# Three column blocks of the samples' token tile: high and low parts side by side as weights

## The chip, the cores and the metric

The kernel runs on one core of one Trainium2 chip. The metric is the device time of one execution in microseconds. Engines are named as in the profile: PE (TensorE, matmuls) with PEld (its weight loads), DVE (VectorE), ACT (ScalarE), POOL (GpSimd), SP (SyncE, which issues most transfers).

## The reference

One layer of a decoder trunk is applied to a prompt of 1024 positions and to a group of 8 samples with 8 positions each, with the same weights, in float32.

```python
h = rmsnorm(x, norm_mix)
q, k, v, gu, gv, ga, gb = split_in(h @ w_in)          # 1024 -> 1024|256|256|768|768|1024|1024
o = sliding-window attention of q, k, v (sinks, window 128)
vn = layernorm(gelu(gv), ln_g, ln_b)                  # an output for the samples
s = gelu(gu) * (causal 128x128 mix of vn per channel group + bias)
merged = sigmoid(ga) * (o @ w_pa) + sigmoid(gb) * (s @ w_pb)
x = x + merged @ w_out
x = x + conv_ffn(rmsnorm(x, norm_ffn))                # up 5632, causal conv 3, gelu gate, down
y = rmsnorm(x, norm_final)
```

Of the input projection, the columns v (256) and gv (768) are needed with tokens on the partitions: v for the attention's second product and for the caches, gv for the LayerNorm over its 768 channels.

## The kernel before

The 64 sample rows and 1024 prompt rows stand as columns: activations are kept transposed, with 128 channels on the partitions and tokens along the row. Every float32 operand of a large product is split into a high part, rounded to TensorE's fast float32 type, and a low part, the rest (`split`, `scale_split`: a cast on ACT, a subtraction on DVE). A product then takes three passes: high by high, high by low, low by high; low by low is left out.

The tokens form two groups. Group 0 has the 64 samples and prompt rows 0 to 511 (576 columns), group 1 the other 512 prompt rows. `hs[k]` holds group 0's normalised input without the row factor (high and low part, 576 columns) for each of the eight 128-channel chunks k. Eight such pairs lie in the first three of four tile pairs `txa[0][kk]`; the fourth pair is written only after group 0's blocks, by `split0(3)`.

The blocks v and gv (as gv0, gv1, gv2, of 256 columns each) are computed with tokens as TensorE's weights and the split weight columns (`wide[key]`, tiles `w2h`, `w2l`, two slots) as the moving operand, so that a result tile has 128 tokens on the partitions and 256 columns. Group 0 has five token tiles, the first named "s" at column 0: it takes 128 columns, of which the first 64 are the samples and the rest prompt rows 0 to 63, which the next tile computes as well. The kernel uses the first 64 rows of it alone. Group 1 has four.

The order at the start is: gv0 of group 0, chunk by chunk as input and weights arrive (`mm_tok` for all five tiles of a chunk, L612); then `tokens(0, "gv1")`, `tokens(0, "v")`, `tokens(0, "gv2")`, and for group 1 v, gv2, gv0, gv1. After the first tile of gv1, `stats_first` computes the row factors `rstg[0]` (a matmul of summed squares with ones at L475, DVE at L257, POOL's power at L258, and diagonals on DVE at L484), and applies Gelu to gv0's five banks. After every token tile one of a list of jobs runs on ACT and DVE: squares, group 1's normalised rows (`norm1`), sums and splits for the later products. A tile's bank (`bank()`, seven of them in turn) is read by ACT in `v_out` or `gv_out`, with the row factor as scale, and stored to DRAM (`gvd`, `vsd`).

Later, while the rest of the input projection runs (seven products in place of eight of 2x2 blocks, `Chain.product`, L300), `ln_load`, `ln_stats` and `ln_out` take the gv rows back from DRAM, one token tile after another, normalise them and store them by channel group (`vnd`) for the mix; the samples' 64 rows also go to the output `gvs`.

Each engine works through its own instructions in order. The instruction order of an engine is set when the program is built, from the order of the code and a planner's idea of when operands are ready; it is not strictly that of the code. Transfers are issued by SP and ACT.

Of the kernel before, what the change touches and what calls it, by code (L numbers as in the profile page):

```python
# [6 lines left out]
F32 = mybir.dt.float32  # L7
F32R = mybir.dt.float32r
I32 = mybir.dt.int32
AF = mybir.ActivationFunctionType  # L10
ALU = mybir.AluOpType
# [4 lines left out]
P = 128  # L16
D = 1024
KD = 8
NS = 64
# [6 lines left out]
GW = 768  # L26
# [8 lines left out]
def layer(tc, a):  # L35
    nc = tc.nc
    V, S, G, PE = nc.vector, nc.scalar, nc.gpsimd, nc.tensor

    def split(hi, lo, src):
        S.copy(hi, src)  # L40
        V.tensor_sub(lo, src, hi.bitcast(F32))  # L41
# [5 lines left out]
    with ExitStack() as top:  # L47
# [19 lines left out]
        eps, warm, mhalf, sign = two[:, 0:1], two[:, 1:2], two[:, 2:7], two[:, 7:8]  # L67
# [252 lines left out]
        def pick(x, place, lo, hi):  # L320
# [3 lines left out]
        groups = [dict(g=0, n=576, off=0, soff=NS, base=192, mbase=448, blk0=0,  # L324
                       chunks=[(192, 0, 320), (512, 320, 576)],
                       toks=[("s", 0), *((i, NS + P * i) for i in range(4))]),
                  dict(g=1, n=512, off=576, soff=0, base=0, mbase=0, blk0=4,
                       chunks=[(0, 0, 256), (256, 256, 512)], toks=[(4 + i, P * i) for i in range(4)])]
# [15 lines left out]
        gvd = {name: dr(f"gvd{name}", [P, GW]) for gr in groups for name, _ in gr["toks"]}  # L344
        vnd = [dr(f"vnd{gr['g']}", [P, NG, len(gr["toks"]), P]) for gr in groups]
# [12 lines left out]
        with ExitStack() as ph1:  # L358
            c1 = ph1.enter_context(tc.tile_pool(name="c1", bufs=1))

            def const1(name, shape, dt=F32):
                t = c1.tile(shape, dt, name="c_" + name)
                nc.sync.dma_start(t, a[name])
                return t
# [6 lines left out]
            late = {}  # L371

            def load_late():
                nc.sync.dma_start(ident, a["ident"])
                late["mprev"] = const1("mprev", [P, 1, P], I32)
                late["sinkb"] = const1("sinkb", [P, NH])
                late["sinks"] = const1("sinks", [P, NKV])
                neg = c1.tile([P, 1], F32, name="c_neg")
                V.memset(neg, NEG)
                late["neg"] = neg  # L380
                w2 = c1.tile([NS, NG, NS], F32, name="c_wss")
                w2r = stg.tile([P, 576], F32, name="stg")[:NS, :NG * NS]
                nc.sync.dma_start(w2r, a["wss"])
                m2 = stg.tile([P, 576], F32, name="stg")[:NS, :NG * NS].bitcast(I32)
                nc.sync.dma_start(m2, a["mss"])
                w2f = w2.rearrange("p a b -> p (a b)")
                V.memset(w2f, 0.0)
                V.copy_predicated(w2f, m2, w2r)
                late["wss"] = w2

            wide = {}
# [71 lines left out]
            rstg = [c1.tile([P, len(gr["toks"])], F32, name=f"rst{gr['g']}") for gr in groups]  # L463
# [40 lines left out]
            gvp = pa0.enter_context(tc.tile_pool(name="gvp", bufs=3))  # L504
            wide["pool"] = pa0.enter_context(tc.tile_pool(name="wide", bufs=2))
            gap(wide["pool"], 192)
            hs, txa = [], [{}, {}]
# [15 lines left out]
            def part1(t, k, lo):  # L523

                return t[:, 5 + lo // 256 if k > 3 else 4 * (lo // 256), lo % 256:lo % 256 + P]

            def mm_tok(ps, g, lo, w, k):
                wh, wl = w
                ah, al = ((part1(t, k, lo) for t in txa[1][k % 4]) if g else (t[:, lo:lo + P] for t in hs[k]))
                for i, (u, v) in enumerate(((ah, wh), (ah, wl), (al, wh))):  # L530
                    PE.matmul(ps, u, v[:, k, :], start=k + i == 0,  # L531
                              stop=k == KD - 1 and i == 2)

            def v_out(g, i, ps):
                name = groups[g]["toks"][i][0]
                v = gvp.tile([P, 256], F32, name="gv")
                S.activation(v, ps, AF.Copy, scale=1.0 if g else rstg[g][:, i:i + 1])
                if name == "s":
                    nc.sync.dma_start(vsd, v[0:NS])
                    for b in range(8):  # L540
                        nc.sync.dma_start(a["vsn"][b], v[8 * b:8 * b + 8])
                else:
                    if name == 4:
                        late["v"] = gvp.tile([P, 256], F32, name="gv")
                        nc.sync.dma_start(late["v"], v3d)
                    for to, x in ((vd, v), (dvd, None)):
                        if x is None and name == 0:
                            continue
                        t = W.sm.tile([P, 4, P], F32, name="ws", bufs=2)
                        tr, four = t.bitcast(F32R), lambda y: y.rearrange("p (h d) -> p h d", d=64)  # L550
                        if x is None:
                            x = t[:, :, 64:128]
                            V.tensor_sub(x, four(v), four(late["v"]))
                            scale_split(tr[:, :, 0:64], tr[:, :, 64:128], x, sign)
                        else:
                            split(tr[:, :, 0:64], tr[:, :, 64:128], four(x))
                        nc.sync.dma_start(to[name], t)
                    late["v"] = v
                    if name == 3:
                        nc.sync.dma_start(v3d, v)  # L560
                if name == 7:
                    nc.sync.dma_start(a["vp"], v)

            def gv_out(g, i, p3, ps, v=None):
                if v is None:
                    v = gvp.tile([P, 256], F32, name="gv")
                S.activation(v, ps, AF.Gelu_apprx_tanh, scale=1.0 if g else rstg[g][:, i:i + 1])
                nc.scalar.dma_start(gvd[groups[g]["toks"][i][0]][:, 256 * p3:256 * p3 + 256], v)

            def tokens(g, key, out, jobs, new=True, after=None):  # L570
                if new:
                    W.get()
                    W.get()
                for i, (_, lo) in enumerate(groups[g]["toks"]):
                    ps = bank()[:, :256]
                    for k in range(KD):
                        mm_tok(ps, g, lo, wide[key], k)
                    if after and i == 0:
                        after()
                    out(i, ps)  # L580
                    if jobs:
                        jobs.pop(0)()
# [16 lines left out]
            ps = bank()  # L599
# [18 lines left out]
                    V.tensor_add(rsg[0], xk[0] if k == 1 else rsg[0], x)  # L618
            with tc.issue_after(dma.ins):
                load_late()  # L620
            rows, first_gv = {}, []

            def stats_first():
# [117 lines left out]
            lnv, lnm = {}, {}  # L741

            def ln_load(n):
                if n < len(lnn):
                    if "lnp" not in late:
                        lnp = late["lnp"] = poola("ln", 1, lno)
                        for x in ("lng", "lnb"):
                            late[x] = lnp.tile([P, GW], F32, name=x)
                            nc.sync.dma_start(late[x], a[x])
                    g, i = lnn[n]  # L750
                    lnv[n] = late["lnp"].tile([P, GW], F32, name="v", bufs=4)
                    nc.sync.dma_start(lnv[n], gvd[groups[g]["toks"][i][0]])

            def ln_stats(n):
                lnp, v = late["lnp"], lnv[n]
                bs_ = lnp.tile([P, 2, 6], F32, name="bst", bufs=2)
                for e in range(2):
                    V.bn_stats(bs_[:, e], v[:, e * 384:e * 384 + 384])
                mv = lnm[n] = lnp.tile([P, 3], F32, name="mv", bufs=3)
                V.bn_aggr(mv[:, 0:2], bs_)  # L760
                V.tensor_scalar(mv[:, 2:3], mv[:, 1:2], EPS, None, ALU.add)
                G.tensor_tensor(mv[:, 2:3], mv[:, 2:3], mhalf[:, 0:1], ALU.pow)

            def ln_out(n):
                (g, i), v, mv = lnn[n], lnv.pop(n), lnm.pop(n)
                V.scalar_tensor_tensor(v, v, mv[:, 0:1], late["lng"], ALU.subtract, ALU.mult)
                V.scalar_tensor_tensor(v, v, mv[:, 2:3], late["lnb"], ALU.mult, ALU.add)
                nc.sync.dma_start(vnd[g][:, :, i], v.rearrange("p (g c) -> p g c", c=P))
                if groups[g]["toks"][i][0] == "s":
                    nc.sync.dma_start(a["gvs"], v[0:NS])  # L770

            def ln_half(n, e):
                def go():
# [625 lines left out]
            for c in range(KD):  # L1399
                for at, go in enumerate(merge(1, c, operand(1)) if c > 1 else [none, none, *first[c][2:]]):  # L1400
                    if at == 1:
                        t, u = held.pop(c)
# [36 lines left out]
            for c in range(KD):  # L1439
                xt = x_next(0, c)  # L1440
                w, ps = W.get(), acc2()
# [66 lines left out]
            for c in range(KD):  # L1508
                xt = x_next(1, c)
                w, ps = W.get(1 if c < 7 else 4), acc2()  # L1510
# [490 lines left out]
```

## Time and profile before

| | |
|---|---|
| median of 3 runs | 1510.91 us (1510.36 to 1510.93) |
| profiled execution | 1509.93 us, of which span 1508.2 us |
| PE busy | 1493.7 us, 99% of the span, 12190 matmuls |
| DVE busy | 1158.7 us, 77% |
| ACT busy | 825.9 us, 55% |
| POOL busy | 265.8 us, 18% |
| mean transfer rate | 190 GB/s |
| mean granted clock of TensorE | 0.998 |

A row of the order of time has the start in us from the span's beginning, the duration, the engine, the line of the kernel, the operation, output tile and input tiles, shapes and a count (rows of like instructions in sequence are merged); in brackets stands how long the engine sat idle before it and what ended that. Rows of waits have the waiting engine, tile and line, the one it waited for, total us, times, and the longest. Rows of windows have the stretch, its length, the busy time and count of instructions running in it, the granted clock, the share of the transfer engines and GB/s. Rows of groups have a count, the busy time with the mean in ns of one, and the idle time before them. A row of one line's instructions gives the shortest, median and longest duration in ns. A matmul's duration is its latency: matmuls overlap, and the distance of their starts is what counts.

### The profile page before, as it was taken

To read this page: it belongs to the slowest core of one execution; us is meant where nothing else is said; L and a number is where in the kernel's file an instruction comes from. 1 tells how busy PE (TensorE), PEld (TensorE's weight loads), DVE (VectorE), ACT (ScalarE), POOL (GpSimd) and SP (SyncE) were. 2 spreads that over 40 slices of the span, in tenths; PEclk is the share of its full clock that TensorE was granted. 3 is DMA by queue.
4 is the path that set the end of the run, shared out by engine and by line. 5 is a ranking of instruction groups with operands and counts; after the bars stand their busy time and mean duration, and the time that the engine had idled before them with its cause. 6 is when DMAs were issued, how large, how long until landed. Compare 5 with 4: busy or idle time off the path is not lost.

```text
span 1508.2 us, 31375 instructions
## 1 busy us (share of the span) xinstructions
PE 1493.7 (99%) x12190; PEld 1481.7 (98%) x12190; DVE 1158.7 (77%) x1909; ACT 825.9 (55%) x1755; POOL 265.8 (18%) x422
## 2 busy tenths in 40 slices
PE   9999999999999999999999999999999999999997
PEld 9999999999999999999999999999999999999997
DVE  6896778756645995989668888898899888785685
ACT  6665764544543774874434555555555556453463
POOL 0000012200120331530222322322132122000002
PEclk9999999999999999999999999999999999999999
DMA  8452457637749757849978333332233226973453
GB/s 289 157 188 112 179 177 265 228 126 271 243 167 333 249 181 224 254 160 322 342 257 282 129 115 122 117 117 107 98 136 109 91 74 219 367 259 97 123 183 133
DMA packets 137508, 286.70 MB, mean 190 GB/s; under 512 B 15248, under 2 KB 44368, under 8 KB 137360
## 3 DMA queue, kind: packets, MB, share of 16 engines
q1 hardware_dynamic: 132352, 279.97, 55.2%
q10 hardware_dynamic: 5008, 4.73, 0.9%
q8 instruction: 96, 1.57, 0.4%
q14 instruction: 52, 0.43, 0.1%
HBM read 195.76 MB, written 90.85 MB: 190 GB/s over the span
## 4 chain that ended last, share of the span: by engine, by line
PE 76%; DVE 5%; ACT 2%; issue 1%; DMA 1%; POOL 0%; DVEq 0%; ACTq 0%; POOLq 0%
PE st L300 41%; PE dn L1740 15%; PE mm L240 14%; PE sc L1233 1%; PE mx L841 1%; PE po L1294 1%; ACT s L1256 1%; DVE s L1259 1%; DVE s L1243 1%; DVE nm L1249 1%; PE pt L1266 1%; DVE of L1305 0%; DVE wl L41 0%; DVE pl L41 0%; DMA v<-gvd 0%
## 5 line engine op out<-in xcount | busy, mean ns | idle before, releaser
L300 PE MATMUL st<-th,wh 128*128 128x256 f32 (+1 forms) x2128 | 610.6, 287 | 1.2 <-ACT ku L283 0.8
L300 PE MATMUL st<-tl,wh 128*128 128x256 f32 (+1 forms) x2128 | 608.7, 286 | 0.0
L300 PE MATMUL st<-th,wl 128*128 128x256 f32 (+1 forms) x2128 | 608.2, 286 | 0.0
L300 PEld LDWEIGHTS st<-th,wh 128*128 128x128 f32 x2128 | 399.9, 188 | 2.6 <-ACT k L281 1.2
L300 PEld LDWEIGHTS st<-th,wl 128*128 128x128 f32 x2128 | 400.3, 188 | 0.0
L300 PEld LDWEIGHTS st<-tl,wh 128*128 128x128 f32 x2128 | 399.7, 188 | 0.0
L40 ACT CAST wh<-wraw 128x512 fp32r<-128x512 f32 (+2 forms) x204 | 139.4, 694 | 99.7 <-PE st L300 35.3
L41 DVE TENSOR_TENSOR wl<-wraw,wh 128x512 fp32r<-128x512 f32 (+2 forms) x204 | 158.5, 790 | 40.2 <-ACT wh L40 38.3
L1740 PE MATMUL dn<-th,wh 128*128 128x288 f32 (+1 forms) x616 | 176.7, 287 | 0.0
L1740 PE MATMUL dn<-tl,wh 128*128 128x288 f32 (+1 forms) x616 | 176.2, 286 | 0.0
L1740 PE MATMUL dn<-th,wl 128*128 128x288 f32 (+1 forms) x616 | 175.1, 284 | 0.0
L40 ACT CAST wh<-ws 128x512 fp32r<-128x512 f32 x160 | 98.1, 622 | 99.8 <-PE st L300 65.5
L41 DVE TENSOR_TENSOR wl<-ws,wh 128x512 fp32r<-128x512 f32 x160 | 111.1, 707 | 44.1 <-ACT wh L40 42.1
L1740 PEld LDWEIGHTS dn<-th,wl 128*128 128x128 f32 x616 | 115.8, 188 | 0.0
L1740 PEld LDWEIGHTS dn<-tl,wh 128*128 128x128 f32 x616 | 115.7, 188 | 0.0
L1740 PEld LDWEIGHTS dn<-th,wh 128*128 128x128 f32 x616 | 115.6, 188 | 0.0
L288 POOL TENSOR_TENSOR z<-ku,k 128x256 f32<-128x256 f32 (+1 forms) x32 | 29.5, 926 | 316.7 <-ACT ku L283 315.4
L41 DVE TENSOR_TENSOR tl<-traw,th 128x544 fp32r<-128x544 f32 (+1 forms) x85 | 61.4, 730 | 22.9 <-ACT th L40 22.8
L40 ACT CAST th<-traw 128x544 fp32r<-128x544 f32 (+1 forms) x85 | 53.8, 642 | 43.9 <-PE dn L1740 28.6
L240 PE MATMUL mm<-s,wh 128*128 128x256 f32 (+1 forms) x384 | 76.7, 294 | 0.0
L531 PE MATMUL st<-w2h,th 128*128 128x256 f32 x308 | 74.5, 283 | 0.2 <-DVE w2l L165 0.2
L240 PE MATMUL mm<-oh,wh 128*128 128x256 f32 (+1 forms) x256 | 73.5, 288 | 0.2
(300 smaller groups left out, 3157.9 us busy)
## 6 DMA issues: line engine op xcount, KB each, us to landing
wraw<-wt SPq DMA_DIRECT2D x133, 512.0 KB
traw<-td SPq DMA_DIRECT2D x77, 272.0 KB
td<-za SPq DMA_DIRECT2D x22, 544.0 KB
wraw<-wt SPq DMA_DIRECT2D x35, 256.0 KB
upd<-hl SPq DMA_DIRECT2D x14, 512.0 KB
td<-t SPq DMA_DIRECT2D x11, 544.0 KB
qd<-q SPq DMA_DIRECT2D x8, 576.0 KB
q<-qd SPq DMA_DIRECT2D x8, 576.0 KB
```

The source lines that it names most:

```text
L40: S.copy(hi, src)
L41: V.tensor_sub(lo, src, hi.bitcast(F32))
L240: PE.matmul(ps[:, lo:lo + c1 - c0], u[:, k, :], v[:, c0:c1], start=(clear and k == 0 and i == 0), stop=(k == nk - 1 and i == 2), skip_grou ...
L288: op(to, pick(x, to, lo, hi), pick(y, to, lo, hi))
L300: PE.matmul(ps, u[:, kk, :], v, start=first and kk + i == 0, stop=kk == 3 and i == 2, skip_group_check=True)
L531: PE.matmul(ps, u, v[:, k, :], start=k + i == 0, stop=k == KD - 1 and i == 2)
L841: PE.matmul(ps[:, P * i:P * i + P], vn[:, i], late["wst"][:, c, :], start=True, stop=True)
L1233: PE.matmul(ps[:, h, o0:256], q, kst[kv][:, e, k0:cur + P], start=e == 0, stop=e == 1)
L1243: V.copy_predicated(s[:, :, 0:P], late["mprev"].to_broadcast([P, 4, P]), ps[:, :, 0:P])
L1249: V.tensor_reduce(nm, s, AX.X, ALU.max, negate=True)
L1256: S.activation(s[:, h], s[:, h], AF.Exp, bias=nm[:, h:h + 1], accum_out=dn[:, h:h + 1])
L1740: PE.matmul(place(m, e), u[:, m, :], v[:, lo:hi], start=new and i + k == 0 and (e == 0 or m % 2 == 0), stop=i == NU - 1 and k == 2, skip_g ...
```

## The change

The samples' tile of three column blocks (gv1, v and gv2 of group 0; gv0 stays) takes other weights: a tile `pair_s` of 8 chunks x 128 columns, in which columns 0 to 63 are the high parts of the 64 samples and columns 64 to 127 the low parts. POOL fills it with sixteen copies of 128x64 from `hs`; it lies in the high tile of the pair `txa[0][3]`. The tile is computed in two passes (by the weights' high part and by their low part) in place of three. Its result has the samples' high-part rows on partitions 0 to 63 and their low-part rows on 64 to 127: `joined` copies the upper rows from PSUM to partitions 0 to 63 on ACT and adds the lower ones on DVE. ACT's activation then reads the sum, on 64 partitions. The sample tile's transfers to and from DRAM and its LayerNorm instructions are cut to 64 rows. The low-by-low product is now part of these three blocks for the samples.

```diff
+            def joined(ps):
+
+                t = gvp.tile([P, 256], F32, name="gv")[0:NS]
+                S.copy(t, ps[NS:P])
+                V.tensor_add(t, t, ps[0:NS])
+                return t
+
             def v_out(g, i, ps):
                 name = groups[g]["toks"][i][0]
-                v = gvp.tile([P, 256], F32, name="gv")
-                S.activation(v, ps, AF.Copy, scale=1.0 if g else rstg[g][:, i:i + 1])
+                if name == "s":
+                    v = joined(ps)
+                    S.activation(v, v, AF.Copy, scale=rstg[g][0:NS, i:i + 1])
+                else:
+                    v = gvp.tile([P, 256], F32, name="gv")
+                    S.activation(v, ps, AF.Copy, scale=1.0 if g else rstg[g][:, i:i + 1])
...
             def gv_out(g, i, p3, ps, v=None):
-                if v is None:
+                name = groups[g]["toks"][i][0]
+                m = NS if name == "s" else P
+                if name == "s" and p3:
+                    v = ps = joined(ps)
+                elif v is None:
                     v = gvp.tile([P, 256], F32, name="gv")
-                S.activation(v, ps, AF.Gelu_apprx_tanh, scale=1.0 if g else rstg[g][:, i:i + 1])
-                nc.scalar.dma_start(gvd[groups[g]["toks"][i][0]][:, 256 * p3:256 * p3 + 256], v)
+                S.activation(v[0:m], ps[0:m], AF.Gelu_apprx_tanh, scale=1.0 if g else rstg[g][0:m, i:i + 1])
+                nc.scalar.dma_start(gvd[name][0:m, 256 * p3:256 * p3 + 256], v[0:m])
...
-                for i, (_, lo) in enumerate(groups[g]["toks"]):
+                for i, (name, lo) in enumerate(groups[g]["toks"]):
                     ps = bank()[:, :256]
                     for k in range(KD):
-                        mm_tok(ps, g, lo, wide[key], k)
+                        if name != "s":
+                            mm_tok(ps, g, lo, wide[key], k)
+                            continue
+                        for e in range(2):
+                            PE.matmul(ps, pair_s[:, k], wide[key][e][:, k, :], start=k + e == 0,
+                                      stop=k == KD - 1 and e == 1)
...
             with tc.issue_after(dma.ins):
                 load_late()
+            pair_s = txa[0][3][0].rearrange("p j c -> p (j c)")[:, 0:KD * P].rearrange("p (k c) -> p k c", c=P)
+            for k, x in enumerate(hs):
+                for e in range(2):
+                    G.tensor_copy(pair_s[:, k, 64 * e:64 * e + 64], x[e][:, 0:NS])
...
-                    lnv[n] = late["lnp"].tile([P, GW], F32, name="v", bufs=4)
-                    nc.sync.dma_start(lnv[n], gvd[groups[g]["toks"][i][0]])
+                    m = NS if groups[g]["toks"][i][0] == "s" else P
+                    lnv[n] = late["lnp"].tile([P, GW], F32, name="v", bufs=4)[0:m]
+                    nc.sync.dma_start(lnv[n], gvd[groups[g]["toks"][i][0]][0:m])
...
```

`ln_stats` and `ln_out` are cut to the same `m` partitions in each of their instructions, and `ln_out` stores 64 rows of `vnd` for the samples' tile.

More of the change, by code (lines that the diff above doesn't have):

```diff
@@ L750, in ln_load @@
                     g, i = lnn[n]
-                    lnv[n] = late["lnp"].tile([P, GW], F32, name="v", bufs=4)
-                    nc.sync.dma_start(lnv[n], gvd[groups[g]["toks"][i][0]])
+                    m = NS if groups[g]["toks"][i][0] == "s" else P
+                    lnv[n] = late["lnp"].tile([P, GW], F32, name="v", bufs=4)[0:m]
+                    nc.sync.dma_start(lnv[n], gvd[groups[g]["toks"][i][0]][0:m])
             def ln_stats(n):
                 lnp, v = late["lnp"], lnv[n]
-                bs_ = lnp.tile([P, 2, 6], F32, name="bst", bufs=2)
+                m = v.shape[0]
+                bs_ = lnp.tile([P, 2, 6], F32, name="bst", bufs=2)[0:m]
                 for e in range(2):
                     V.bn_stats(bs_[:, e], v[:, e * 384:e * 384 + 384])
-                mv = lnm[n] = lnp.tile([P, 3], F32, name="mv", bufs=3)
+                mv = lnm[n] = lnp.tile([P, 3], F32, name="mv", bufs=3)[0:m]
                 V.bn_aggr(mv[:, 0:2], bs_)
                 V.tensor_scalar(mv[:, 2:3], mv[:, 1:2], EPS, None, ALU.add)
-                G.tensor_tensor(mv[:, 2:3], mv[:, 2:3], mhalf[:, 0:1], ALU.pow)
+                G.tensor_tensor(mv[:, 2:3], mv[:, 2:3], mhalf[0:m, 0:1], ALU.pow)
             def ln_out(n):
                 (g, i), v, mv = lnn[n], lnv.pop(n), lnm.pop(n)
[L766 to L770, printed above, removed]
+                m = v.shape[0]
+                V.scalar_tensor_tensor(v, v, mv[:, 0:1], late["lng"][0:m], ALU.subtract, ALU.mult)
+                V.scalar_tensor_tensor(v, v, mv[:, 2:3], late["lnb"][0:m], ALU.mult, ALU.add)
+                nc.sync.dma_start(vnd[g][0:m, :, i], v.rearrange("p (g c) -> p g c", c=P))
+                if m == NS:
+                    nc.sync.dma_start(a["gvs"], v)
             def ln_half(n, e):
```

## The prediction

> **What bounds the kernel now.** I read the page's busy table and slices first, then TensorE's waits, then windows and the order of time in the stage that the edit touches.
>
> ```profile
> span 1508.2 us, 31375 instructions
> PE 1493.7 (99%) x12190; PEld 1481.7 (98%) x12190; DVE 1158.7 (77%) x1909; ACT 825.9 (55%) x1755; POOL 265.8 (18%) x422
> PE   9999999999999999999999999999999999999997
> PEclk9999999999999999999999999999999999999999
> ```
> ```profile
> PE st L601 <- DVE c_ones L75: 1.2, 1, 1.2
> PE po L1294 <- ACT s L1241: 1.1, 1, 1.1
> ...
> PE st L300 <- ACT ku L283: 0.8, 1, 0.8
> PE fs L1775 <- ACT sq L1759: 0.6, 1, 0.6
> PE st L531 <- ACT tl L44: 0.6, 1, 0.6
> ...
> PE st L531 <- DVE w2l L165: 0.2, 1, 0.2
> ```
>
> TensorE is the bound in every slice, and its longest wait anywhere is 1.2 us. So a matmul that goes is worth its spacing in the stream, wherever it stands, and time saved early is kept: no later stage has a large wait that would soak it up. By the same rows a delay of TensorE's start is paid in full.
>
> The page's 276 to 287 ns of one matmul are latency; the spacing comes from windows.
>
> ```profile
> 14.59:21.17 6.58, 6.58 (x59) 1.00 0.98 295
> ...
> 46.80:115.10 68.30, 68.30 (x583) 1.00 0.56 181
> ```
>
> The first window has 58 starts beside one matmul already running: 6.58 / 58 = 0.113 us. The second, the same kind of matmul for most of it, gives 68.30 / 581 = 0.118 us at the same granted clock of 1.00.
>
> **The terms that leave.** The samples' tile has 8 chunks in three passes, 24 matmuls; now 16. Three column blocks (gv1, v, gv2 of group 0) lose 8 each; gv0 keeps its three passes. The tiles of gv1 and v stand where the spacing is 0.113: 8 x 0.113 = 0.91 us each. That of gv2 starts near 53 us, where it is 0.118: 0.94 us. Sum 2.76 us, or 0.18%. The number of columns loaded as weights stays 128, so the weight loads go with their matmuls and cost nothing apart.
>
> **What comes in at the start: sixteen copies on POOL.** The side-by-side tile is filled from the split rows of chunk k, two copies of 128x64 each. POOL itself has the room:
>
> ```profile
> 25.52 1.17 POOL L258 TENSOR_TENSOR rst<-rst,c_eps 128x5 f32<-128x5 f32 x1 [24.49 <-DVE rst L257]
> ```
>
> It sits idle for 24.49 us before its first real instruction. The nearest copies of that length are at L913 (64 elements in a row), some with VectorE idle, some with it busy:
>
> ```profile
> L913 POOL COPY qs<-stg x16: 229/234/742, 439.2 to 445.1; 64x64 f32<-64x64 f32 x16
> ...
> 439.25 2.15 POOL L913 COPY qs<-stg 64x64 f32<-64x64 f32 x8 [1.48 <-PE st L300]
> 441.44 4.33 POOL L913 COPY qs<-stg 64x64 f32<-64x64 f32 x8
> 441.54 0.69 DVE L41 TENSOR_TENSOR wl<-wraw,wh 128x512 fp32r<-128x512 f32 x1 [3.06 <-ACT wh L40]
> 442.32 0.69 DVE L41 TENSOR_TENSOR wl<-ws,wh 128x512 fp32r<-128x512 f32 x1
> 443.05 0.69 DVE L179 TENSOR_TENSOR ws<-ws,wraw 128x512 f32<-128x512 f32 x1
> ...
> 63.41 0.68 DVE L41 TENSOR_TENSOR tl<-wh,th 128x512 fp32r<-128x512 f32 x1
> 64.01 0.42 DVE L669 SCALAR_TENSOR_TENSOR wl<-stg,wh 128x256 f32<-128x256 f32 x1
> ```
>
> Alone, eight copies take 2.15 us, 0.27 each. Beside VectorE subtractions of two SBUF operands the next eight take 4.33 us. The subtractions pay too: their starts are 441.54, 442.32, 443.05, so 0.78 and 0.73 us apart, where 63.41 to 64.01 shows 0.60 with POOL idle. A copy that slips in between two such instructions costs VectorE 0.13 to 0.18 us.
>
> That matters because VectorE, not TensorE, gates the first tile of gv1:
>
> ```profile
> 10.40 0.81 DVE L45 SCALAR_TENSOR_TENSOR tl<-wh,c_gains,tl 128x576 fp32r<-128x576 f32 x1
> ...
> 13.73 0.81 DVE L45 SCALAR_TENSOR_TENSOR tl<-wh,c_gains,th 128x576 fp32r<-128x576 f32 x1
> ...
> 16.59 0.81 DVE L45 SCALAR_TENSOR_TENSOR tl<-wl,c_gains,th 128x576 fp32r<-128x576 f32 x1
> 17.32 0.75 DVE L618 TENSOR_TENSOR rs<-rs,wh 128x576 f32<-128x576 f32 x1
> 18.17 0.76 DVE L618 TENSOR_TENSOR rs<-rs,wl 128x576 f32<-128x576 f32 x1
> 18.85 2.35 DVE L41 TENSOR_TENSOR w2l<-wraw,w2h 128x1024 fp32r<-128x1024 f32 x2
> 21.12 0.75 DVE L618 TENSOR_TENSOR rs<-rs,wh 128x576 f32<-128x576 f32 x1
> ```
> ```profile
> 14.60 0.39 PE L531 MATMUL st<-w2h,tl 128*128 128x256 f32 x1
> ...
> 21.18 0.28 PE L531 MATMUL st<-w2h,th 128*128 128x256 f32 x1
> 21.29 0.35 PE L531 MATMUL st<-w2l,th 128*128 128x256 f32 x1
> ```
>
> From 10.4 us VectorE runs without a gap: low parts of h for chunks 2 to 7 (10.40 is chunk 2, 13.73 chunk 4, 16.59 chunk 7), sums of squares, and at 18.85 the two halves of gv1's low weights, done at 21.20. TensorE reads them with the tile's second matmul, at 21.29: no slack. The new tile has the same order (high weights first, low second) and waits for the same instruction.
>
> All of these subtractions have two SBUF operands. Copies of chunks 0 and 1 fall before 10 us, where VectorE waits for others. Those of chunks 2 to 7, twelve, become ready between about 10.4 and 19 us, one or two per chunk, and go in one per gap between VectorE's instructions; from 10.40 to the second half at 18.85 there are fourteen such gaps, so I let all twelve in. The cost is 12 x 0.13 = 1.6 to 12 x 0.18 = 2.2 us; I take 12 x 0.15 = 1.8. Ends of the unknown: nothing, if the copies find gaps; 12 x 0.23 = 2.8, if VectorE loses each copy's whole duration (0.23 is the L913 copies' median). Part of it shows at 14.60 already, where TensorE follows chunk 4's low part by 0.06 us: five copies earlier, 0.75 us. That delay lies inside the 1.8, since the weights come later still.
>
> [...]
>
> **What else comes in.** The tile's result is joined: ACT copies rows 64 to 127 of PSUM, VectorE adds rows 0 to 63, then ACT's activation on 64 rows as before. So ACT waits for VectorE once per block, with its next Gelu or cast behind it, and VectorE waits for ACT, with its next split behind it.
>
> ```profile
> L281 ACT COPY k<-st 128x256 f32<-128x256 f32 x76 | 27.5, 366 | 9.1 <-PE st L300 8.6 <-ACT gv L567 0.4
> ...
> 445.59 0.41 DVE L288 TENSOR_TENSOR z<-ku,st 128x256 f32<-128x256 f32 x1
> ...
> 26.72 0.84 ACT L567 ACTIVATE wl<-st,rst 128x256 f32<-128x256 f32 x2 [3.77 <-POOL rst L258]
> ...
> 33.09 1.23 DVE L41 TENSOR_TENSOR w2l<-wraw,w2h 128x1024 fp32r<-128x1024 f32 x1 [5.34 <-ACT w2h L40]
> ...
> 67.22 0.28 PE L531 MATMUL st<-w2h,th 128*128 128x256 f32 x1
> ```
>
> That is 0.37 and 0.41 us per block. In gv1 it lies in ACT's 3.77 us of idleness before 26.72 and VectorE's 5.34 before 33.09: nothing. In v and gv2 it lies beside TensorE's stream. The next thing that TensorE needs is group 1's operands: the last splits of its normalised rows are at 63.41 (done 64.09), used from 67.22, a cover of 3.1 us; three added blocks of 0.8 us at most, in an engine pair that recovers between them, and TensorE arriving 1 us earlier, leave it covered. If that cover were gone, the excess would be paid one to one. The bank of the tile is asked for again seven tiles later: nothing.
>
> The scratch tile for the pair is the fourth high tile of group 0, whose own contents are written after group 0's blocks; nothing waits. The sample tile's rows written to and read from DRAM halve (ACT's and SP's queues carry as many transfers, smaller), and the LayerNorm instructions run on 64 partitions with the same elements per partition: nothing.
>
> **Sum.** +1.8 - 0.91 - 0.91 - 0.94 = -0.96 us. The profiled execution took 1509.93 us (span 1508.2 and 1.7 around it) and would take about 1509.0; the median of the runs shown, 1510.91, is 0.98 above it, and moves to 1509.95.
>
> **Rivals.**
> - *The copies cost VectorE nothing on the path* (they find gaps, or VectorE yields nothing). For it: half the copies at L913 ran at 0.27. Against: the 0.73 and 0.78. Then -2.76: 1508.15. Chance 0.20.
> - *VectorE loses each copy in full*: 2.8 - 2.76, no change, 1510.95. For it: the eight copies' doubling; against: the spacing. Chance 0.18.
> - *TensorE's spacing between 46 and 115 us changes.* The 0.118 sets in with no wait and no clock change behind it, so a shifted start may fall on 0.113: 581 x (0.1176 - 0.1134) = 2.4 us more gained, 1507.5. Against: nothing in the order of matmuls there changes. Chance 0.10.
> - *POOL starves, and the new tile waits for its copies: slower.* If VectorE's unbroken run kept POOL out, the twelve copies would start in its first gap, near 24.4 us, and be done 12 x 0.27 = 3.3 us later; the tile would end near 27.9 instead of 23.99, +3.9, then -0.91 - 0.94: +2.05, 1512.95. It decides for slower once gv1's tile starts over 2.76 us late. Against: at 441.44 to 443.05 one copy got in per subtraction. Chance 0.07.
> - Forecast 0.42; another order of the work on ACT and VectorE, either way, 0.03.
>
> **How the numbers follow.** 0.2% is 3.02 us, about what a measurement of this kernel can tell from no change; the whole gain of the matmuls is below it. Faster by more: the spacing's rival, and the first rival with a little besides, 0.10 + 0.04. Slower by more: starvation worse than worked out, and the unnamed, 0.04 + 0.03. The rest, 0.79, is within. The range runs from the first rival to somewhat above the second, 1508.0 to 1511.6: with the forecast these hold 0.80.
>
> **What the profile would show.** Right: gv1's first sample matmul near 22 us and its second near 23.1, with a wait of TensorE for w2l at L41 of about 1 us; VectorE's 128x576 instructions 0.85 to 0.9 us apart between 10 and 20 us, instead of 0.73; POOL copies of 0.6 to 0.8 us there; 16 matmuls in each of three sample tiles; group 1's first matmul near 66.2. Wrong: gv1's sample tile starting by 21.4 (first rival), a wait of TensorE for a POOL copy (starvation), or another spacing after 46 us. A new wait of TensorE in v or gv2 for a bank or for group 1's operands would mean that joining the rows was not covered.

## The result: 2.6 us slower, and the profile after

The changed kernel took 1513.99 us (median of 13 executions, 1511.05 to 1515.74), the kernel before beside it 1510.66 us (13, 1509.05 to 1512.43). The ratio is 1.0017, 95% interval [1.0010, 1.0024]: by the ratio 2.6 us slower (the medians lie 3.3 us apart), where 0.96 us faster was forecast. Two later comparisons of the same two kernels gave 1.0014 [1.0004, 1.0023] and 1.0016 [1.0006, 1.0025].

The profiled execution of after took 1515.74 us, the upper end of its range, while that of before, 1509.93, stood 0.7 below its median; so the two traces lie 5.8 us apart, more than the medians. First the page's busy table:

```profile
span 1514.0 us, 31353 instructions
PE 1495.1 (99%) x12166; PEld 1481.9 (98%) x12166; DVE 1159.4 (77%) x1912; ACT 829.7 (55%) x1758; POOL 277.3 (18%) x438
```

Then the longest of TensorE's waits in the same execution (waiting engine, tile and line, releaser: total us, times, longest):

```profile
PE st L531 <- DVE w2l L41: 2.6, 1, 2.6
...
PE sc L1168 <- issue: 0.7, 1, 0.7
```

The 24 matmuls are gone (12166 against 12190), POOL has its 16 copies more (438 against 422), ACT and DVE 3 more each. New is a wait of TensorE of 2.6 us for the low weights `w2l` at L41. Before, no wait for them at that line is listed; the 0.2 us for `w2l` in the list of before is of L165, at the kernel's start. TensorE in the order of time around it (start, duration, engine, line, tiles; in brackets the idle time before and its releaser):

```profile
98.17 0.28 PE L531 MATMUL st<-w2h,tl 128*128 128x256 f32 x1
98.70 0.38 PE L531 MATMUL st<-w2h,th 128*128 128x256 f32 x1 [0.25 <-ACT w2h L40]
101.69 0.38 PE L531 MATMUL st<-w2l,th 128*128 128x256 f32 x1 [2.61 <-DVE w2l L41]
...
102.41 0.42 PE L531 MATMUL st<-w2h,tl 128*128 128x256 f32 x1
102.62 0.41 PE L531 MATMUL st<-w2h,th 128*128 128x256 f32 x1
...
105.18 0.41 PE L531 MATMUL st<-w2h,th 128*128 128x256 f32 x1
105.40 0.32 PE L531 MATMUL st<-w2l,th 128*128 128x256 f32 x1
105.56 0.28 PE L531 MATMUL st<-w2h,tl 128*128 128x256 f32 x1
105.68 0.28 PE L531 MATMUL st<-w2h,th 128*128 128x256 f32 x1
```

This is group 1's last column block, gv1, with its weights split anew. TensorE waits there for the second half of `w2l`, and then its matmuls stand 0.21 us apart until 105.4 us, instead of 0.12. The windows show the granted clock (length; busy us and count of PE, PEld, DVE, ACT, POOL; granted clock, transfer share, GB/s):

```profile
101.00:104.00 3.00, 2.31 (x12) 2.31 (x13) 3.00 (x5) 0.99 (x3) 0.00 (x0) 0.68 0.67 202
104.00:107.00 3.00, 3.00 (x22) 3.00 (x22) 3.00 (x8) 2.45 (x5) 0.00 (x0) 0.76 0.30 115
```

So in this execution the stage costs twice: the wait itself, and then some 16 spacings of 0.211 instead of 0.118, another 1.5 us.

Where does the time go? I set the start of each TensorE matmul against the start of the same matmul in the trace before (negative: earlier). All kernels of this study, each explained further down, stand in one table, the columns being times of the trace before (101.2 is the last matmul ahead of the first that needs the second half of `w2l`). The last two columns are of that block and the start of the next stage alone:

| kernel | 56 us | 101.2 | 122 | 300 | 480 | end | wait for `w2l` | half clock behind a wait near 100 to 116 us |
|---|---|---|---|---|---|---|---|---|
| after | -2.85 | -2.44 | +1.67 | +2.99 | +4.01 | +5.3 | 2.6 | 3.4 us |
| again | -3.07 | -2.94 | +1.17 | +1.95 | +2.72 | +2.8 | 2.6 | none |
| again2 | -3.24 | -3.24 | +0.11 | +0.76 | +1.56 | +3.3 | 2.0 | none |
| swap | -2.69 | -2.69 | +3.85 | +3.48 | +4.59 | +4.8 | 0.3 | 6.8 us |
| third | -0.43 | -0.43 | +0.35 | +0.21 | +1.53 | +1.3 | under 0.2 | none |
| twice | +2.61 | +2.61 | +7.03 | +7.41 | +8.51 | +11.2 | 2.5 | 3.4 us |
| drop | -3.53 | -3.53 | -0.13 | -0.06 | +0.03 | +0.3 | 1.8 | 3.4 us |
| buf4 | -2.93 | -2.93 | -3.17 | -3.80 | -2.95 | -1.8 | under 0.2 | none |
| buf4_2 | -1.82 | -1.81 | -0.79 | +0.72 | +1.53 | +2.4 | under 0.2 | none |
| dropb | -2.09 | -2.09 | -2.32 | -3.71 | -3.70 | -2.6 | under 0.2 | none |
| buf4b | -0.32 | -0.32 | -0.26 | -1.34 | -1.24 | +1.0 | under 0.2 | none |
| rows64 | +0.05 | +0.05 | +0.03 | -1.07 | -1.07 | 0.0 | under 0.2 | none |

By 56 us the change has given what its matmuls are worth, 2.85 us (2.76 was worked out). It keeps that until 98 us, and by 104 us stands 2.1 us behind. One traced execution differs from the next: rows64, which hardly changes anything, shifts by 1.1 us and back, and after, again and again2, one and the same kernel, end up to 2.5 us apart. So single entries beyond 122 us say less than the step between 101.2 and 122.

### The profile page after: what moved, and what is told of

Same layout as the page of the kernel before. It is cut to its first block, busy times and chain, and to the rows that moved or that the text cites. A ratio compares the mean times of both kernels' runs of the same rounds, so it can differ in the third digit from the quotient of the medians.

```text
span 1514.0 us, 31353 instructions
## 1 busy us (share of the span) xinstructions
PE 1495.1 (99%) x12166; PEld 1481.9 (98%) x12166; DVE 1159.4 (77%) x1912; ACT 829.7 (55%) x1758; POOL 277.3 (18%) x438
## 3 DMA queue, kind: packets, MB, share of 16 engines
q8 instruction: 95, 1.56, 0.4%
## 4 chain that ended last, share of the span: by engine, by line
PE 87%; DVE 8%; ACT 2%; DMA 2%; issue 1%; SPq 0%; DVEq 0%; ACTq 0%
PE st L300 50%; PE dn L1767 15%; PE mm L240 14%; PE st L531 3%; PE sc L1260 1%; ACT s L1283 1%; PE mx L868 1%; DVE s L1286 1%; DMA gvd<-gv 1%; PE po L1321 1%; DVE wl L41 1%; DVE tl L41 1%; DVE s L1270 1%; DVE nm L1276 1%; DVE of L1332 0%
## 5 line engine op out<-in xcount | busy, mean ns | idle before, releaser
L41 DVE TENSOR_TENSOR wl<-wraw,wh 128x512 fp32r<-128x512 f32 (+2 forms) x204 | 160.2, 798 | 36.0 <-ACT wh L40 34.1
L41 DVE TENSOR_TENSOR wl<-ws,wh 128x512 fp32r<-128x512 f32 x160 | 109.2, 695 | 50.8 <-ACT wh L40 49.2
L41 DVE TENSOR_TENSOR tl<-traw,th 128x544 fp32r<-128x544 f32 (+1 forms) x85 | 61.3, 730 | 22.4 <-ACT th L40 22.3
L240 PE MATMUL mm<-ol,wh 128*128 128x256 f32 (+1 forms) x256 | 74.1, 290 | 0.0
```

The source lines that it names most:

```text
L240: PE.matmul(ps[:, lo:lo + c1 - c0], u[:, k, :], v[:, c0:c1], start=(clear and k == 0 and i == 0), stop=(k == nk - 1 and i == 2), skip_grou ...
```

## Who makes the weights late

The weights `w2l` are a VectorE subtraction behind a cast on ACT. First the trace before, then the trace after, ACT and DVE between 82 and 102 us:

```profile
90.63 0.38 ACT L567 ACTIVATE gv<-st 128x256 f32<-128x256 f32 x1 [2.81 <-DMA gvd<-gv]
...
94.91 2.00 ACT L40 CAST w2h<-wraw 128x1024 fp32r<-128x1024 f32 x2
96.74 2.35 DVE L41 TENSOR_TENSOR w2l<-wraw,w2h 128x1024 fp32r<-128x1024 f32 x2
101.25 0.28 PE L531 MATMUL st<-w2l,th 128*128 128x256 f32 x1
```
```profile
83.10 0.34 ACTq L583 DMA_DIRECT2D gvd<-gv  x1
84.53 0.68 ACT L40 CAST th<-wh 128x576 fp32r<-128x576 f32 x1 [1.46 <-DVE wh L720]
89.43 0.39 ACT L582 ACTIVATE gv<-st 128x256 f32<-128x256 f32 x1 [4.23 <-DMA gvd<-gv]
...
93.48 0.39 ACT L582 ACTIVATE gv<-st 128x256 f32<-128x256 f32 x1 [2.02 <-DMA gvd<-gv]
...
94.88 1.04 ACT L40 CAST w2h<-wraw 128x1024 fp32r<-128x1024 f32 x1
95.81 0.67 ACT L40 CAST th<-wh 128x576 fp32r<-128x576 f32 x1
97.02 0.68 ACT L40 CAST th<-wl 128x576 fp32r<-128x576 f32 x1 [0.53 <-DVE wl L693]
97.60 1.04 ACT L40 CAST w2h<-wraw 128x1024 fp32r<-128x1024 f32 x1
...
96.90 1.22 DVE L41 TENSOR_TENSOR w2l<-wraw,w2h 128x1024 fp32r<-128x1024 f32 x1
...
100.41 1.22 DVE L41 TENSOR_TENSOR w2l<-wraw,w2h 128x1024 fp32r<-128x1024 f32 x1
```

Before, both halves were done at 96.74 + 2.35 = 99.09 and needed at 101.25: 2.2 us to spare, less than the 2.85 us by which TensorE now comes earlier. But the weights came later as well, at 100.41 + 1.22 = 101.63. Two things on ACT stand ahead of this; the runs below show which of them counts. Gelu writes gv rows into a ring of three buffers (`gvp`), and ACT writes a buffer again only when its store to DRAM has landed: the Gelus at 89.43 and 93.48 us each start 0.08 us behind a landing (89.35, 93.40). Two of the three still hold v rows here, whose difference DVE takes at 91.59 (L564), so Gelu has one in effect. TensorE delivers earlier, and the store goes out 1.9 us earlier (83.10; before at 85.04), but by the semaphores of its sixteen transfer engines it lands at 89.35, only 1.2 us before the 90.55 of the trace before; the next one, issued at 89.84, lands at 93.40. ACT stands still for 4.2 + 2.0 us instead of 2.8, with every cast queued behind. And the two halves of the weights, next to each other before, now have split0(2)'s casts between them (on DVE 98.41 to 100.41). The instruction orders are fixed when the program is built, and the order after differs from that before.

## The experiments

**rows64.** The kernel before with the LayerNorm's cut alone.

```diff
-                S.activation(v, ps, AF.Gelu_apprx_tanh, scale=...)
-                nc.scalar.dma_start(gvd[name][:, 256 * p3:...], v)
+                S.activation(v[0:m], ps[0:m], AF.Gelu_apprx_tanh, scale=...)
+                nc.scalar.dma_start(gvd[name][0:m, 256 * p3:...], v[0:m])
```

> The kernel before with the cut to 64 rows alone (the samples' Gelu, transfers and LayerNorm instructions of gv; three passes as before). Every theory: no new wait of TensorE and a time within 1 us of before.

Measured in one profiled execution: 1509.94 us, end shift 0.0, no new wait. The trace shows neither a cost nor a gain of the cut, as the prediction had it; one execution can't tell a microsecond.

**twice.** The changed kernel with POOL's copies done twice over.

```diff
-                for e in range(2):
+                for e in (0, 1, 0, 1):
                     G.tensor_copy(pair_s[:, k, 64 * e:64 * e + 64], x[e][:, 0:NS])
```

> Each of the sixteen copies is made twice. By the prediction's price (0.13 to 0.18 us of VectorE per copy between two subtractions) the low weights of group 0's gv1 would be done about 2 us later than in the changed kernel, near 23.1 us, and gv1's second matmul would wait that long. By the changed kernel's trace (about 0.02 us per copy) they are done within 0.5 us of 21.1, unless POOL itself finishes its copies after TensorE asks for them.

One profiled execution took 1521.08 us. POOL's copies in the order of time:

```profile
18.38 2.40 POOL L644 CAST th<-th 128x64 fp32r<-128x64 f32 x2
...
22.33 2.03 POOL L644 CAST th<-th 128x64 fp32r<-128x64 f32 x3
24.30 0.54 POOL L644 CAST th<-tl 128x64 fp32r<-128x64 f32 x2
```

And one of TensorE's waits:

```profile
PE st L596 <- POOL th L644: 1.9, 2, 1.5
```

VectorE was not late: gv1's tile reached its low weights at 20.74 us, 0.5 us earlier than in the trace before. The cost showed at POOL itself, whose last copies ended near 24.8 us and for which TensorE then waited 1.9 us; 6.8 us at half the granted clock followed, from 25.6 us on. The copies' price for VectorE, the disputed term, is thereby nearly nothing, and the prediction's fourth rival (the tile waits for POOL) is real once the copies are doubled. In the kernel as changed they were done at 18.9 us, before TensorE's 20.98.

**swap.** In the list of jobs after each token tile, split0(2) and the empty job behind it change places, so that the casts for gv1's second half are queued ahead.

```diff
-                    ..., split0(1), both(x_in(3), sums0(2)), split0(2),
-                    none, both(ahead(1), sums0(3)), ...
+                    ..., split0(1), both(x_in(3), sums0(2)), none,
+                    split0(2), both(ahead(1), sums0(3)), ...
```

> One entry of the list of jobs moves: split0(2) and the empty job behind it change places, so that both halves of gv1's weights for group 1 stand ahead of that split in the code. Theory (the order that the planner made of ACT's and VectorE's work puts the second half behind other splits): the wait of 2.6 us falls under 0.7 us, no half clock follows, and the time is 3 to 4.5 us under the changed kernel's, 1508 to 1510. Rival (TensorE arrives 2.85 us early at a stage that transfers and ACT's waits hold to its own time, whatever the order): the wait stays above 2 us and the time at 1512 to 1515.

Measured: 1515.07 us, above the 1508 to 1510 expected, ratio to before 1.0019 [1.0009, 1.0029]. TensorE's waits in its profile:

```profile
PE st L300 <- ACT k L281: 3.6, 2, 3.4
...
PE st L531 <- DVE w2l L41: 0.3, 1, 0.3
```

Its windows behind that wait:

```profile
112.00:116.00 4.00, 0.96 (x9) 0.75 (x7) 3.97 (x8) 3.60 (x10) 0.00 (x0) 0.94 0.66 182
116.00:119.00 3.00, 2.65 (x12) 2.65 (x13) 1.60 (x3) 0.57 (x2) 0.00 (x0) 0.50 0.61 238
119.00:122.50 3.50, 3.50 (x19) 3.50 (x18) 0.42 (x1) 0.37 (x1) 0.00 (x0) 0.52 0.00 0
```

The wait for `w2l` is down to 0.3 us as meant, and the lead is lost some 14 us later, in a wait of 3.4 us for ACT's first copy of the next stage, with 6.8 us of half clock around and behind it. ACT is no later there than in the changed kernel, whose first copy of that stage came at 116.54, 116.03 and 114.98 us in three executions (after, again, again2). The rows of swap, then of again:

```profile
115.92 0.65 ACT L281 COPY k<-st 128x256 f32<-128x256 f32 x2 [0.40 <-ACT gv L582]
...
116.03 0.65 ACT L281 COPY k<-st 128x256 f32<-128x256 f32 x2 [0.40 <-ACT gv L582]
```

So ACT comes there about as late in both, and TensorE, where it has not lost its lead to the weights, loses it to the copy. The order of the two halves decides where the lead is lost, not whether. My theory that the order was the cause fell here.

**third.** The changed kernel with a third matmul per chunk, so that TensorE has no lead.

```diff
-                        for e in range(2):
-                            PE.matmul(ps, pair_s[:, k], wide[key][e][:, k, :], start=k + e == 0,
-                                      stop=k == KD - 1 and e == 1)
+                        for e in range(3):
+                            PE.matmul(ps, pair_s[:, k], wide[key][e % 2][:, k, :], start=k + e == 0,
+                                      stop=k == KD - 1 and e == 2)
```

> The samples' tile gets a third matmul per chunk again (the high weights a second time, so that this product is counted twice): TensorE has as many matmuls as before, all else is the changed kernel's. If TensorE's lead is what uncovers the weights, the wait at group 1's gv1 falls to 0 to 0.5 us, without half clock, and the time is 1510.5 to 1511.5. If the weights come late by the order alone, moving with TensorE, the wait stays at 2 us or more and the time is 1514 to 1518.

In the profile TensorE does not wait for these weights at all without the lead, and ACT's store wait is back to one, of 3.0 us; so far the first of the two expectations holds. Its time does not: 1514.97 us, from 1511.6 to 1520.6, ratio 1.0025 [1.0012, 1.0039]. With as many matmuls as before and no lead to lose, the changed kernel is still slower than before. The profiled execution, 1511.73, was near the low end, so what the others lost is not seen.

**drop.** The other way round: the kernel before with the lead and nothing added.

```diff
-                        mm_tok(ps, g, lo, wide[key], k)
+                        mm_tok(ps, g, lo, wide[key], k, 2 if g + i == 0 else 3)
```

> The kernel before, in which the samples' tile of gv1, v and gv2 leaves out its third pass (the samples' low parts by the high weights): 24 matmuls fewer, and nothing added: no copies on POOL, no joining, no 64-row tiles. Theory (the lead itself is lost at the stage's end): TensorE is 2.7 us ahead near 56 us and loses 2 us or more of it by 116 us in waits for gv1's low weights or for the first product's bank; 1510 to 1514. Rival (the added instructions of the change are what delays ACT and VectorE): no wait, and 1508 to 1509, 2.7 us under before.

Measured: 1512.64 us, ratio 1.0004 [0.9992, 1.0015]. Twenty-four matmuls less, and no gain that the interval shows. From its profile, TensorE's longest wait and ACT's:

```profile
PE st L531 <- DVE w2l L41: 1.8, 1, 1.8
...
ACT gv L567 <- DMA gvd<-gv: 5.4, 2, 3.4
```

And the windows there:

```profile
98.00:101.00 3.00, 1.32 (x9) 1.33 (x10) 3.00 (x5) 0.36 (x3) 0.00 (x0) 0.93 0.70 190
101.00:104.00 3.00, 3.00 (x16) 3.00 (x15) 3.00 (x8) 2.46 (x5) 0.00 (x0) 0.50 0.73 288
```

A lead of 3.5 us at 101.2 is 0.1 at 122. This is the cleanest run of the study: no copies on POOL, no joined rows, and the lead is lost at the same place. With three buffers for gv rows, the lead itself can't pass this stage.

**buf4 and buf4b.** A fourth buffer for gv rows, so that ACT need not wait for the stores, in the changed kernel (buf4) and in the kernel before (buf4b). The room for it comes from loading the mask `c_wss` in `mix_first` instead of at the start.

```diff
-            gvp = pa0.enter_context(tc.tile_pool(name="gvp", bufs=3))
+            gvp = pa0.enter_context(tc.tile_pool(name="gvp", bufs=4))
...
-                w2 = c1.tile([NS, NG, NS], F32, name="c_wss")     # at the start
+                w2 = mp.tile([NS, NG, NS], F32, name="c_wss")     # in mix_first
```

> The changed kernel with four gv buffers in place of three (the mask tile c_wss, which stood in that room, is loaded later). In the changed kernel ACT stood still 4.2 and 2.0 us near 89 and 93 us, until stores of earlier gv tiles had landed, with the casts of gv1's weights behind it. Theory (those waits make the end of the token stage late, so that TensorE's lead of 2.85 us is lost there): with a fourth buffer they fall under 1 us together, TensorE's waits at gv1's low weights and at the first product's bank (115 us in the time of before) fall under 0.7 us together, and the time is 1.5 to 3 us under before, 1508.5 to 1510. Rival (the amount of work of ACT and VectorE alone makes the stage late): the waits of TensorE stay at 2 us or more together, 1512 to 1515.

> The kernel before with the same four gv buffers and the later mask, without the change. Both theories: TensorE hardly waited in this stage before, so the time stays within 1 us of before; a gain here as large as that of the changed kernel with four buffers would say that the buffers, not TensorE's lead with the buffers, are what counts.

Measured side by side on one chip: buf4 1510.32 us, ratio to before 0.9991 [0.9979, 1.0003]; buf4b 1513.48 us, 1.0005 [0.9993, 1.0017]. The buffer with the later mask shows no gain in the kernel before; in the changed one it takes the loss away. The expected time, 1508.5 to 1510, was missed by 0.3 us. The window 84 to 90 us of after:

```profile
84.00:90.00 6.00, 6.00 (x53) 6.00 (x52) 3.01 (x7) 1.06 (x2) 0.00 (x0) 1.00 0.93 296
```

The same window of buf4:

```profile
84.00:90.00 6.00, 6.00 (x53) 6.00 (x53) 5.24 (x11) 3.05 (x8) 0.00 (x0) 1.00 0.86 313
```

And of buf4 ACT and DVE in the order of time, and TensorE where it takes up the second half of these weights:

```profile
89.77 1.04 ACT L40 CAST w2h<-wraw 128x1024 fp32r<-128x1024 f32 x1
92.33 1.05 ACT L40 CAST w2h<-wraw 128x1024 fp32r<-128x1024 f32 x1
...
95.14 1.22 DVE L41 TENSOR_TENSOR w2l<-wraw,w2h 128x1024 fp32r<-128x1024 f32 x1
```
```profile
98.20 0.28 PE L522 MATMUL st<-w2h,th 128*128 128x256 f32 x1
98.32 0.28 PE L522 MATMUL st<-w2l,th 128*128 128x256 f32 x1
```

The transfers are as busy as ever (0.86 against 0.93), but ACT works 3.05 us of the six instead of 1.06, DVE 5.24 instead of 3.01; the weights are done at 96.36 instead of 101.63, 2 us before TensorE asks for them, and the lead passes the stage whole. The two halves still stand apart, with split0(2)'s casts between them, as in the changed kernel: their order was not what cost the time.

**dropb, buf4_2, again2.** Side by side on one chip: drop with the fourth buffer, buf4 once more, and the changed kernel once more. again, earlier, was the first repetition.

> The kernel before with a fourth buffer for gv rows (the mask's load moved to make the room), and with the samples' tile of gv1, v and gv2 of group 0 computed in two passes from the old weights; it leaves out the product of the low parts of the samples by the high weights in these blocks. Nothing of the change is added. Theory (the lead of TensorE is lost because ACT stands still for the landing of gv's stores, and then its casts of group 1's last weights come late): ACT has no wait for those stores over 0.5 us, TensorE waits for gv1's second weights under 0.6 us in the last block of group 1, no half clock there, and a lead of 2.5 to 3.5 us at 56 us of the kernel before is still 2.5 or more at 118 us; time 0.9975 to 0.9990. Rival (the lead is lost whatever ACT does, since the weights and splits behind are bound to the inputs' arrival or to an order that follows TensorE): lead under 1 us at 118 us; time 0.9995 to 1.0010, as without the buffer.

> The changed kernel with a fourth buffer for gv rows, once more and beside the next one on the same chip, since its interval still held no change. Theory: lead of about 2.9 us kept past 118 us, ratio 0.998 to 0.9995, and 2 to 4 us below the changed kernel without the buffer. Rival (the first profile was a lucky one): a wait for gv1's second weights over 1.5 us or a half clock at 98 to 118 us, ratio 1.000 to 1.002.

> The changed kernel unchanged, as the neighbour of the two above. Theory: a wait of TensorE of 2 to 3.5 us for gv1's second weights in group 1's last block, the lead under 0.5 us by 118 us, ratio 1.0010 to 1.0022. Rival (where the lead goes differs from run to run): no such wait in this profile, ratio below 1.0005.

> The changed kernel as it is, for a second profile. If its loss lies in one place, the profile again shows TensorE ahead by 2.5 to 3 us until about 98 us, then one wait of 2 to 3 us for the low part of gv1's weights in group 1 and a stretch of half clock behind it. If instead the loss is the sum of small delays that differ from run to run, that wait is under 1 us here and the time is lost elsewhere. Time 1511 to 1516 us either way.

| kernel | us | ratio to before, 95% |
|---|---|---|
| dropb | 1508.33 | 0.9979 [0.9967, 0.9991] |
| buf4_2 | 1510.19 | 0.9989 [0.9979, 1.0000] |
| again2 | 1514.28 | 1.0016 [1.0006, 1.0025] |
| again (earlier) | 1513.87 | 1.0014 [1.0004, 1.0023] |

dropb is what 24 matmuls less are worth when the lead is kept: 0.21% of 1512 is 3.2 us (1.4 to 5.0 by the interval), against 2.76 worked out. Its lead in the trace is 2.1 us at 56 us, less than the 2.5 expected, since the first weights came 1.1 us late at 6.1 us; but it is kept, 2.3 us at 122. With three buffers the same kernel showed no gain. That shows the cause: the ring of three, in which ACT waits for a store. ACT's order of work from the first cast of these weights to the second is the same in drop and in dropb. buf4_2 is 4.1 us below its neighbour again2. The changed kernel with four buffers (buf4, buf4_2) is the best version that computes the whole layer, with two intervals that end at 1.0003 and 1.0000: a gain of about 1.5 us that is hardly told from none.

Both repetitions of the changed kernel have the wait (2.6 and 2.0 us). Neither has the half clock there, and both then wait 1.4 us at the start of the next stage. So the half clock belongs to single executions and is not the cause; their loss was complete without it.

buf4_2's profiled execution came to 56 us with a lead of 1.8 us, where 2.9 was expected (the first weights were 0.9 us late at 5.9 us), took it through this stage, and unlike buf4's lost it later: 0.7 us at 114 us, 1.0 at 223 and 1.2 at 269 (there 0.8 in before as well). ACT and TensorE at the second of these:

```profile
221.43 0.67 ACT L40 CAST q<-z 128x576 fp32r<-128x576 f32 x1 [2.14 <-DMA kd<-q]
...
222.97 0.40 PE L300 MATMUL st<-th,wh 128*128 128x288 f32 x1 [1.00 <-ACT ku L281]
```

It is the same pattern once more, a store's landing (`kd`) that ACT waits for before it may write the tile again, with TensorE's operand behind it. After has it too, 1.7 us. This one I only read; no run took it away. The rest of what lies between buf4 and dropb, 1.9 us, is open. One piece of it has a place: TensorE's 0.7 us before the first of the samples' scores (L1168 in the table of waits above), in all profiles with the change (third's names POOL's L950 as releaser, the others nothing that the profile shows) and in none without it.

## The prediction, step by step

- **The terms that leave: right.** 2.76 us worked out, 2.7 to 3.2 read at 56 us in the executions of after, again, again2, swap and buf4 (1.8 in buf4_2, which waited at its start), and 3.2 in dropb's time.
- **POOL's copies: the term that was mis-sized.** 1.8 us were put on VectorE's path; the trace shows about 0.25. (Of gaps between VectorE's instructions there are thirteen from 10.40 to the second half of the weights, not fourteen; twelve copies fit either way.) From chunk 2's subtraction to the end of gv1's low weights it took 10.40 to 21.20 = 10.80 us before. After:

```profile
10.06 0.87 DVE L45 SCALAR_TENSOR_TENSOR tl<-wh,c_gains,tl 128x576 fp32r<-128x576 f32 x1
...
18.72 2.39 DVE L41 TENSOR_TENSOR w2l<-wraw,w2h 128x1024 fp32r<-128x1024 f32 x2
...
21.16 0.38 PE L596 MATMUL st<-w2l,th 128*128 128x256 f32 x1
...
4.03 0.24 POOL L644 CAST th<-th 128x64 fp32r<-128x64 f32 x1 [3.00 <-ACT th L44]
...
15.78 0.78 POOL L644 CAST th<-th 128x64 fp32r<-128x64 f32 x1
16.51 0.79 POOL L644 CAST th<-tl 128x64 fp32r<-128x64 f32 x1
```

10.06 to 21.11 is 11.05 us: 0.25 more for twelve copies, 0.02 each. It is POOL that pays: 0.24 us for the copy at 4.03, with VectorE idle, and 0.64 to 0.79 for ten of these twelve, in VectorE's unbroken run (the other two took 0.24 and 0.23). The 0.73 and 0.78 spacings of VectorE at 441 to 443 us, on which the term rested, had another reason: the second subtraction there waits for ACT's cast at 441.67, and the third works on what the second leaves. The same pair stands 0.73 apart with POOL idle as well, at 126.71 and 127.44 in the trace before. I read a dependency as contention. So the first rival (the copies cost nothing on the path) was the right picture of the start. With 0.25 in place of 1.8 the sum would have been -2.51 us, further from the result: this error hid part of the next one.
- **Joining the rows: right as far as TensorE's waits show.** ACT waited for VectorE's addition once visibly (0.75 us at 58.08), and TensorE waits for nothing there.
- **"Time saved early is kept: no later stage has a large wait that would soak it up": the step that failed.** A stage with no wait in the profile is not a stage with room. The 3.1 us of cover were read at group 1's normalised rows, used from 67 us; the weights of group 1's last block, whose second half is needed at 101.25, had 2.2, and were left out of the list. ACT's wait of 2.81 us for a store stood in the trace, off the path of that execution, and sets a floor: drop shows that a lead of 3.5 us is lost there entirely, dropb that it is kept once the store no longer holds ACT.
- **No rival ended there.** The only named one that was slower was POOL starving, which twice shows to be possible, but it was not what happened. "A new wait of TensorE for group 1's operands" stood among the signs that would prove the cover wrong; it came, in gv1 of group 1 and not in v or gv2, and drop shows that it comes without any joining.
- **The spacing after 46 us** stayed at 0.118 (435 starts in the 51.2 us from 46.8 to 98.0, as many as before), so the third rival did not come. From 105.5 to 110, behind the wait, it was 0.114, which gave back 0.4 us by 116.
- **Why slower than before, and not the same as drop: open.** The lost lead by itself accounts for no gain, not for a loss. What the change adds was put at nothing apart from the copies, and it costs something: after stands 1.5 to 2 us above drop by the ratios (1.0014 to 1.0017 against 1.0004; the intervals overlap), buf4_2 1.9 us above dropb, and third, which has no lead to lose, at 1.0025 [1.0012, 1.0039]. Two pieces have a place in the traces: the wait at the next stage's start (1.4 us in again and again2, none in after) and the 0.7 us at the samples' scores. The runs don't divide it further.

## What to carry to other kernels

A saving on the engine that bounds the kernel is kept only if everything that it meets later is earlier by as much: list for each later stage when its operands are ready and when they are needed, and take the smallest of these margins, not that of the nearest stage. Look on the engines that are not the bound for waits on a store's landing before a buffer is written again: they cost nothing today, need not move with the work ahead of them (here by 1.2 us where the issue moved by 1.9), and can swallow the next gain. Before a spacing is booked as contention, see whether the later instruction was waiting for its operand.

## What the runs showed of the hardware that I had not expected

- A wait of TensorE of 2.6 us was followed by 3.4 us at half the granted clock in one execution (after) and by none in another (again); 1.8 us went with 3.4 us in drop, 2.0 with none in again2, 3.4 us with 6.8 us in swap, and 1.9 us in two pieces with 6.8 us in twice. Between 1.8 and 2.6 us the length of the wait did not tell whether a half clock goes with it.
- Copies of 128x64 on POOL beside VectorE's two-operand subtractions took up to 0.79 us instead of 0.24, and cost VectorE 0.25 us for twelve, about 0.02 each.
- A store of 128 KB issued at 83.10 us, with the transfer engines 0.93 busy from 84 to 90, landed at 89.35: 6.2 us, against 1.7 for one issued at 93.90 (landed at 95.59), with the engines 0.23 busy meanwhile. The buffer is held sixteen times as long as the 0.38 us of the Gelu that fills it.
